# A float32 encoder layer in quads of seven products: subtractions and sums of the up projection, and weight splits, on another engine, and three transfers at other times

## The chip, the cores and the metric

The kernel runs on one core of one Trainium2 chip. A core has a matrix engine (TensorE; PE in the profile, PEld for its weight loads), VectorE (DVE), ScalarE (ACT), GpSimd (POOL), and a sync engine (SP) that here only issues DMAs. Each engine takes its own instructions in the order in which they stand and waits at semaphores. The metric is the device time of one execution in microseconds (us): a median over several runs.

## The reference

One layer of an encoder over 2048 tokens of width 1024, all in float32:

```python
h  = rms_norm(x, norm_mix)
z  = h @ w_in                       # 1024 -> 4352: q_A k_A v_A q_B k_B v_B gate_A gate_B
y_a = windowed_gqa(q_a, k_a, v_a, sink)        # 8 heads on 2 key/value heads, |t-s| <= 128
y_b = neighborhood_attn(q_b, k_b, v_b, rpb)    # 8 heads, 8 x 16 neighbours on a 32 x 64 grid
gates = sigmoid([gate_A, gate_B] + b_gate)
x  = x + (gates_A * (y_a @ w_proj_a) + gates_B * (y_b @ w_proj_b)) @ w_out
x  = x + square(relu(rms_norm(x, norm_mlp) @ w_up)) @ w_down
return rms_norm(x, norm_final)
```

The matrix products of `w_up` (1024 x 4096) and `w_down` (4096 x 1024) take about half of the time.

## The kernel before

**Precision.** A float32 operand goes into TensorE as two numbers of the type float32r: a rounded high part and the rest. `split` makes them: ScalarE casts the high part (L280), and another engine subtracts it from the source (L281). `mm3s` then issues three matmuls (L284 high x high, L285 high x low, L286 low x high). For the slices of weights that the dense tiles use, L176 and L177 do the same.

**Quads.** The input projection, `w_up` and `w_down` are done in quads of two by two blocks with seven products instead of eight, after Strassen and Winograd. The sums of blocks that these need are made by `add` (L277). The `w_up` stage is 16 turns, one quad each (half `m` of the tokens by an eighth `q` of the columns), with its products in the order 1, 5, 6, 2, 7, 4, 3, each for two tiles `a`. Products gather in PSUM banks `b`; VectorE adds them to what is there already (`uc<-b,uc`), ScalarE does relu and square, and after product 3 four more sums (`s1`, `a21`, `s2`, `s4`, L277 too) prepare the left operand of `w_down`, which are stored as `at`.

**The stages by time.** Up to about 365 us the input projection for the first two blocks of tokens' features (`zb`, `zwhl`); from there to 640 the windowed attention A, with dense tiles of the projection (`mm<-hT,whl`) between its units; to 1050 the neighbourhood attention B; to 1440 the gates, the two projections and `w_out`; to 2047 `w_up`; then `w_down`.

**What sets the order.** A planner places the instructions on each engine by a model of their durations, and reads the source's order as a wish only; `tc.issue_after(x)` says that what follows may not be issued before `x`. So an edit at one place can change the order in the whole of its stage.

**Homes.** `pools(stack, side, tags, name)` lays the buffers of a stage out from the left or the right end of SBUF, in the order of the tags. A buffer that comes to lie on one of an earlier stage has to wait for the earlier one's last reader.

**What the change touches.** In `in_left` (L362 ff.) the split of seven left parts of a quad of the input projection; `turned_out` in the loop over the quads, which transposes and stores a quarter of the next block's normalised tokens between products; `qk_tile` and `v_tile`, the dense tiles of attention A's and B's queries, keys and values, with `split_slice` (L176 and L177); `load_kv(g, m)` (L720 ff.), the four DMAs that bring half `m` of the keys and values of group `g` back from DRAM; `began`, a list of the DMAs that bring the queries `qa` of each unit of attention A; the homes of the two attentions; and in `w_up` `up_left` (`uwhla`, `uwhlb`), `up_right` (`ubh`) and `up_quad` (the four sums of `uc`).

## Time and profile before

| | |
|---|---|
| median of 3 runs | 2670.79 us (2670.56 to 2671.09) |
| the profiled execution | 2667.52 us; its span 2665.6 us |
| busy share of the span | PE 97%, PEld 81%, DVE 60%, ACT 46%, POOL 27% |
| mean granted TensorE clock | 0.995 |

The profile is of one execution. A row of a group names the source line, the engine, the operation, the tile that is written and those that are read, how often, busy time and mean duration, and then the idle time of the engine ahead of it with what ended it. A row of the waits names what TensorE stood still for. A row of the timeline gives the start in us from the span's start, the duration, and in brackets the idle time before with its releaser. In a row of the windows stand, for a stretch of time, the busy time of each engine with the number of instructions, the granted clock of TensorE, the busy share of the DMA engines, and what they moved.

### The profile page before, as it was taken

The numbers are of one execution on the slowest core, as the hardware profiler recorded it, in microseconds if no ns is written. First come the engines' busy times: TensorE is split into PE (matmuls) and PEld (weight loads), VectorE is DVE, ScalarE is ACT, GpSimd is POOL, SyncE is SP. The second block draws the span as 40 slices with busy tenths as digits, with TensorE's granted clock in tenths as the row PEclk, the third lists the DMA queues.
The fourth block names the chain that finished last, engine by engine and source line by source line (L and its number), as shares of the span: only waits on it lengthen the run. The fifth ranks groups of instructions, "written<-read, shape, count | busy, mean of one in ns | idle before, by whom it ended". The sixth has DMA issues, their size and how long they took to land. (4 is left out here: it accounts for less than half of the span.)

```text
span 2665.6 us, 34671 instructions
## 1 busy us (share of the span) xinstructions
PE 2596.3 (97%) x12140; PEld 2154.9 (81%) x12140; DVE 1597.4 (60%) x2467; ACT 1238.9 (46%) x2265; POOL 722.5 (27%) x605
## 2 busy tenths in 40 slices
...
GB/s 182 200 156 190 139 248 125 116 117 180 217 218 192 185 181 138 308 160 152 186 182 193 210 202 220 281 188 152 157 115 234 338 113 181 145 146 168 186 190 168
DMA packets 352942, 490.29 MB, mean 184 GB/s; under 512 B 27752, under 2 KB 187624, under 8 KB 350592
## 3 DMA queue, kind: packets, MB, share of 16 engines
...
q14 instruction: 78, 0.64, 0.1%
...
## 5 line engine op out<-in xcount | busy, mean ns | idle before, releaser
L285 PE MATMUL b<-dwh,dah 128*128 128x512 f32 x896 | 348.7, 389 | 0.4 <-DVE dwh L281 0.4
L286 PE MATMUL b<-dwh,dah 128*128 128x512 f32 x896 | 347.7, 389 | 0.0
L284 PE MATMUL b<-dwh,dah 128*128 128x512 f32 x896 | 338.5, 389 | 1.7 <-ACT dwh L280 1.7
L280 ACT CAST dah<-da 128x1024 fp32r<-128x1024 f32 (+1 forms) x128 | 120.8, 945 | 367.6 <-PE b L286 244.6
L277 POOL TENSOR_TENSOR uc<-uc,uc 128x512 f32<-128x512 f32 x120 | 239.7, 2012 | 190.9 <-ACT uc L1204 158.4
L281 DVE TENSOR_TENSOR dah<-da,dah 128x1024 fp32r<-128x1024 f32 (+1 forms) x128 | 139.2, 1089 | 219.5 <-ACT dah L280 216.5
L284 PE MATMUL b<-ubh,uwhlb 128*128 128x512 f32 x592 | 230.6, 390 | 2.7 <-DVE uc L277 1.9
L286 PE MATMUL b<-ubh,uwhlb 128*128 128x512 f32 x592 | 229.7, 390 | 2.3 <-POOL uwhlb L281 1.4
L285 PE MATMUL b<-ubh,uwhlb 128*128 128x512 f32 x592 | 230.4, 389 | 0.0
L200 PE MATMUL mm<-hT,whl 128*128 128x512 f32 x544 | 218.4, 402 | 0.0
L202 PE MATMUL mm<-hT,whl 128*128 128x512 f32 x544 | 214.6, 395 | 0.0
L201 PE MATMUL mm<-hT,whl 128*128 128x512 f32 x544 | 214.2, 394 | 0.0
L284 PEld LDWEIGHTS b<-dwh,dah 128*128 128x128 f32 x896 | 168.1, 188 | 37.0 <-ACT dwh L280 2.1
L284 PE MATMUL zb<-zh,zwhl 128*128 128x512 f32 x476 | 186.9, 394 | 10.4 <-DVE zc L277 7.6
L285 PEld LDWEIGHTS b<-dwh,dah 128*128 128x128 f32 x896 | 168.2, 188 | 35.7 <-DVE dwh L281 0.8
L286 PEld LDWEIGHTS b<-dwh,dah 128*128 128x128 f32 x896 | 168.2, 188 | 34.9
L277 DVE TENSOR_TENSOR uc<-b,uc 128x512 f32<-128x512 f32 x160 | 108.6, 687 | 142.1 <-PE b L286 133.3
L285 PE MATMUL zb<-zh,zwhl 128*128 128x512 f32 x476 | 186.5, 392 | 0.0
L286 PE MATMUL zb<-zh,zwhl 128*128 128x512 f32 x476 | 183.5, 392 | 2.6 <-DVE zwhl L281 2.6
L1452 POOL TENSOR_TENSOR st<-st,power 128x1 f32<-128x1 f32 x16 | 13.6, 857 | 614.5 <-DVE st L1451 614.4
L228 POOL TENSOR_TENSOR st<-st,power 128x1 f32<-128x1 f32 x32 | 23.9, 745 | 470.7 <-DVE st L226 470.6
L284 PEld LDWEIGHTS b<-ubh,uwhlb 128*128 128x128 f32 x592 | 111.1, 188 | 27.2 <-issue 3.1
...
## 6 DMA issues: line engine op xcount, KB each, us to landing
...
```

The costliest lines, as they stand in the source:

```text
L200: PE.matmul(ps, lh, rh, start=first, stop=False)
L201: PE.matmul(ps, lh, rl, start=False, stop=False)
L202: PE.matmul(ps, ll, rh, start=False, stop=last)
L228: G.tensor_tensor(out=r, in0=r, in1=power, op=ALU.pow)
L277: return eng.tensor_tensor(out=out, in0=a, in1=b, op=op).ins
L280: A.copy(hi, src)
L281: return eng.tensor_tensor(out=lo, in0=src, in1=hi.bitcast(F32), op=ALU.subtract).ins
L284: PE.matmul(ps, lh, rh, start=first, stop=False, skip_group_check=True)
L285: PE.matmul(ps, lh, rl, start=False, stop=False, skip_group_check=True)
L286: PE.matmul(ps, ll, rh, start=False, stop=last, skip_group_check=True)
L1452: G.tensor_tensor(out=r, in0=r, in1=power, op=ALU.pow)
```

## The change

Eight edits, in the order of the source.

- `in_left`: the low parts of products 4 and 3 are subtracted on VectorE instead of GpSimd (18 of 128x1024 or smaller).
- The quarters of the next tokens are transposed after the products 2 to 5 of quads 5 and 6 rather than 0 to 3.
- The home of `biasa1` goes from the right side to the left.
- `qk_tile(O_KA)` and `v_tile(O_VA)`: the low part of these two weight slices on VectorE.
- `load_kv` takes an instruction that it is issued after; for the second half it is the load of the queries of unit 8 (for group 0) and 11 (for group 1), counted in the order in which the units run.
- The homes of attention B: `kb0` right behind `masks`, and each of the buffers of `qb` and `biass` a home of its own, in another order.
- `w_up`: products 4 and 3 of the left operand (32 subtractions), the second half of the right operand's pages 4 and 3, and all four sums behind product 3 (120 of 128, eight were there already) on VectorE instead of GpSimd.
- `load_y(b + 1)` stands at another place of the dense stage's source.

```diff
--- before.py
+++ after.py
@@ -387,7 +387,7 @@
                 add(V, s2, a22, a21, ALU.subtract)
             elif n == 3:
                 add(V, a12, a12, s2, ALU.subtract)
-            yield parts({1: a11, 2: a12, 5: s1, 6: s2, 7: a21, 4: a22, 3: a12}[n], G if n in (4, 3) else V)
+            yield parts({1: a11, 2: a12, 5: s1, 6: s2, 7: a21, 4: a22, 3: a12}[n], V)
 
     def v_parts(col, b, vt, p2, v2):
 
@@ -636,8 +636,8 @@
             normalised(xp, xt, Junk(), by_scalar=True)
         ops2.extend(lf if q == 2 else ())
         for n, _ in enumerate(quad2 if q == 2 else in_quad(*QUADS[q], iter(lf), right)):
-            if q in (5, 6) and n < 4:
-                turned_out(h1d[b - 2], in_e().rearrange("p k x -> p (k x)"), xt, n)
+            if q in (5, 6) and 2 <= n < 6:
+                turned_out(h1d[b - 2], in_e().rearrange("p k x -> p (k x)"), xt, n - 2)
     s_z.close()
     s_zp.close()
 
@@ -649,8 +649,8 @@
     s_h = ExitStack()
     hpl = [pool(f"hT{n}", side="left", stack=s_h) for n in range(4)]
     s_a = ExitStack()
-    ap_ = pools(s_a, "left", ("ka1", "va1", "qa", "sta", "sa", "ya", "dist", "ph", "pl"), "a")
-    ap_.update(pools(s_a, "right", ("biasa0", "va0", "ka0", "biasa1"), "a"))
+    ap_ = pools(s_a, "left", ("ka1", "va1", "qa", "sta", "sa", "ya", "dist", "ph", "pl", "biasa1"), "a")
+    ap_.update(pools(s_a, "right", ("biasa0", "va0", "ka0"), "a"))
     hp = {}
 
     def h_pages(b):
@@ -676,7 +676,7 @@
     def qk_tile(col, scale, tiled=False):
         raw = load_slice([(cols(w_in[0], col), KC)])
         yield
-        hl = split_slice(raw)
+        hl = split_slice(raw, V if col == O_KA else G)
         yield
         for b in (2, 3):
             ps = psum("mm", 2)
@@ -689,7 +689,7 @@
     def v_tile(col):
         raw = load_slice([(cols(w_in[0], col), KC)])
         yield
-        hl = split_slice(raw)
+        hl = split_slice(raw, V if col == O_VA else G)
         yield
         for b in (2, 3):
             ps = psum("mm", 2)
@@ -717,12 +717,13 @@
     kas = [T(ap_, [P, 2, S], F32R, f"ka{g}", 1) for g in range(2)]
     vas = [T(ap_, [P, 16, P], F32R, f"va{g}", 1) for g in range(2)]
 
-    def load_kv(g, m):
+    def load_kv(g, m, behind=None):
         k, kd = kas[g][:, :, m * (S // 2) : (m + 1) * (S // 2)], ks_a[m][g]
-        SY.dma_start(k[:, 0].bitcast(F32), kd)
-        SY.dma_start(k[0:64, 1].bitcast(F32), kd[64:128])
-        SY.dma_start(k[64:128, 1].bitcast(F32), kd[0:64])
-        SY.dma_start(vas[g][:, 8 * m : 8 * m + 8].bitcast(F32), vs_a[m][g])
+        with tc.issue_after(behind) if behind else nullcontext():
+            SY.dma_start(k[:, 0].bitcast(F32), kd)
+            SY.dma_start(k[0:64, 1].bitcast(F32), kd[64:128])
+            SY.dma_start(k[64:128, 1].bitcast(F32), kd[0:64])
+            SY.dma_start(vas[g][:, 8 * m : 8 * m + 8].bitcast(F32), vs_a[m][g])
 
     def attn_a(g, i):
         c0, c1 = (1 if i == 0 else 0), (2 if i == 15 else 3)
@@ -834,7 +835,7 @@
     paced(fill, range(12), 24, 3)
     flush(queue=SY)
     for g in range(2):
-        load_kv(g, 1)
+        load_kv(g, 1, began[8 + 3 * g])
     drive((attn_a(g, i) for g in range(2) for i in range(7, 16)), live, True)
     paced(fill, range(12, 24), 24, 3)
     del done[:]
@@ -843,10 +844,10 @@
 
 
     s_b = ExitStack()
-    bp = pools(s_b, "right", ("masks", "qb", "braw0", "biass", "stb", "kb0", "biasl", "braw1", "kb1"), "b")
+    bp = pools(s_b, "right", ("masks", "kb0", "qb0", "braw0", "biass0", "stb", "biass1", "qb1", "qb2", "biasl", "braw1", "kb1"), "b")
     bp.update(pools(s_b, "left", ("sb0", "sb1", "sb2", "vb0", "vb1", "vb2", "phb", "plb", "yb"), "b"))
     boff, bstart, btotal = bias_layout()
-    last_exp, n_raw = [None], [0]
+    last_exp, n_raw, n_short = [None], [0], [0]
     yb = T(bp, [P, BT], F32, "yb", 1)
     masks = T(bp, [P, btotal], F32, "masks", 1)
     with tc.issue_after(began[20]):
@@ -856,7 +857,8 @@
     def make_bias_b(h, jt):
         j = (0, 1, 3)[jt]
         w = B_W[j]
-        t = T(bp, [P, 40 * w], F32, "biasl" if jt == 1 else "biass", 1 if jt == 1 else 2)
+        t = T(bp, [P, 1280 if jt == 1 else 1024], F32, "biasl" if jt == 1 else f"biass{n_short[0] % 2}", 1)[:, : 40 * w]
+        n_short[0] += jt != 1
         raw = T(bp, [P, 512], F32, f"braw{(n_raw[0] + 1) % 2 if n_raw[0] > 1 else 0}", 1)[:, : 16 * w]
         n_raw[0] += 1
         first = h * T_ROWS * w + (T_RO - 11) * w + (B_C0[j] - 16 * j - 15 + T_COFF[j])
@@ -886,7 +888,7 @@
         e, t = h % 2, h // 2
         w, jt = B_W[j], JT[j]
         kp = 4 * w
-        q = T(bp, [P, 4, P], F32R, "qb", 3)
+        q = T(bp, [P, 4, P], F32R, f"qb{n_u % 3}", 1)
         SY.dma_start(q.bitcast(F32), qs_b[t][e][:, :, j])
         yield
         v = T(bp, [P, 8, P], F32R, f"vb{n_u % 3}", 1)
@@ -1099,9 +1101,9 @@
         out[6] = parts(s2, V)
         out[2] = parts(a12, V)
         out[7] = parts(a21, V)
-        out[4] = parts(a22, G)
+        out[4] = parts(a22, V)
         add(V, a12, a12, s2, ALU.subtract)
-        out[3] = parts(a12, G)
+        out[3] = parts(a12, V)
         return out
 
     h2s_d = {n: dp.tile([BT, BT], F32, name=f"h2sum{n}") for n in (5, 6, 7, 4)}
@@ -1146,8 +1148,8 @@
 
         def parts(n, src):
             hi, lo = up_page[n](), up_page[n]()
-            for s, h, l, e in zip(halves(src), halves(hi), halves(lo), (V, G if m and n in (4, 3) else V)):
-                last = split(s, h, l, e)
+            for s, h, l in zip(halves(src), halves(hi), halves(lo)):
+                last = split(s, h, l, V)
             right[n] = (hi, lo)
             page_done[0] = last
 
@@ -1253,14 +1255,13 @@
                     last = plus(a21, ps, a21)
                     squared(a21)
                     s1, s2, s4 = up_rings["c"](), up_rings["c"](), up_rings["c"]()
-                    e = V if m == 1 and q == 7 else G
-                    add(e, s1, a21, a22)
+                    add(V, s1, a21, a22)
                     keep(5, a, s1)
-                    add(e, a21, a11, a21, ALU.subtract)
+                    add(V, a21, a11, a21, ALU.subtract)
                     keep(7, a, a21)
-                    add(e, s2, s1, a11, ALU.subtract)
+                    add(V, s2, s1, a11, ALU.subtract)
                     keep(6, a, s2)
-                    add(e, s4, a12, s2, ALU.subtract)
+                    add(V, s4, a12, s2, ALU.subtract)
                     keep(3, a, s4)
             if last:
                 with tc.issue_after(last):
@@ -1330,6 +1331,8 @@
         for t in range(4):
             row0 = b * BT + t * P
             xt = load_tile(p4x, "xr", 5, xf[row0 : row0 + P])
+            if t == 1 and b < NB - 1:
+                next_y = load_y(b + 1)
             for c in range(2):
                 xc = xt[:, c * BT : (c + 1) * BT]
                 ps = psum("pt", 2)
@@ -1341,8 +1344,6 @@
             put(x2d[b][t * P : (t + 1) * P], xt)
             tiles.append(xt)
         flush()
-        if b < NB - 1:
-            next_y = load_y(b + 1)
         normalised(p4x, tiles, Unused())
     h2 = T(p4x, [P, KC, BT], F32R, "mh", 1).bitcast(F32)
     for g in range(4):
```

In instruction rows VectorE goes from 2442 to 2613 and GpSimd from 508 to 334. TensorE's order is the same from the middle of the first turn of `w_up` on to the end, and in the whole dense stage from about 1050 to 1440 us, where the orders of the other engines are the same too; the last edit moves nothing there. The places where it changes are around 74 to 130, 215 to 295, 353 to 433 and 640 to 880 us and at the start of `w_up`. Three of them are shown.

SP's queue, around 385 to 400 us, where attention A's units begin. `ka0` and `ka1` are the keys of the two groups, `ks_a0` and `ks_a1` the first and second half of them in DRAM, `qa_...` a unit's queries. Before:

```order
L735 DMA qa_322_3116<-qs_a10_78 128x4x128
L686 DMA ks_a1_81<-z_432_3918 64x2x512 x2
L735 DMA qa_332_3187<-qs_a10_78 128x4x128
L686 DMA ks_a1_81<-z_433_3948 64x2x512 x2
L722 DMA ka0_291_2936<-ks_a1_81 128x1024
L723 DMA ka0_291_2936<-ks_a1_81 64x1024
L187 DMA raw_444_4095<-in_w_in_dram 128x8x128
L724 DMA ka0_291_2936<-ks_a1_81 64x1024
L722 DMA ka1_292_2937<-ks_a1_81 128x1024
L723 DMA ka1_292_2937<-ks_a1_81 64x1024
L735 DMA qa_342_3258<-qs_a10_78 128x4x128
```

Now:

```order
L736 DMA qa_332_3187<-qs_a10_78 128x4x128
L736 DMA qa_342_3258<-qs_a10_78 128x4x128
L686 DMA ks_a1_81<-z_433_3948 64x2x512 x2
L187 DMA raw_444_4095<-in_w_in_dram 128x8x128
L736 DMA qa_352_3329<-qs_a10_78 128x4x128
L173 DMA y_a1_103<-ya_321_3113 64x4x128
L736 DMA qa_363_3405<-qs_a00_76 128x4x128
L701 DMA vs_a1_83<-z_437_3986 128x2x512
L736 DMA qa_373_3476<-qs_a00_76 128x4x128
L723 DMA ka0_291_2936<-ks_a1_81 128x1024
L724 DMA ka0_291_2936<-ks_a1_81 64x1024
L725 DMA ka0_291_2936<-ks_a1_81 64x1024
```

The loads of the second half's keys stood ahead of `qa_342` and `qa_352`; now four more loads of queries stand ahead of the first of them, and those of `ka1` come some dozen rows later still.

VectorE's queue around 346 to 360 us, the end of the input projection: `hT` are the pages of normalised tokens for the dense tiles, `zc` the sums that empty the PSUM banks `zb`, `zwhl` and `whl` weights. Before:

```order
L667 SCALAR_TENSOR_TENSOR hT_287_2921<-raw_288_2922,g_mix_68,hT_286_2920 128x512 x2
L667 SCALAR_TENSOR_TENSOR hT_287_2921<-raw_289_2928,g_mix_68,hT_286_2920 128x512 x2
L277 TENSOR_TENSOR zc_278_2707<-zb_76_2694,zc_274_2621 128x512
L277 TENSOR_TENSOR zc_279_2722<-zb_77_2709,zc_275_2636 128x512
L667 SCALAR_TENSOR_TENSOR hT_299_2948<-raw_300_2949,g_mix_68,hT_298_2947 128x512 x2
L277 TENSOR_TENSOR zc_280_2736<-zb_76_2694,zc_274_2621 128x512
L277 TENSOR_TENSOR zc_280_2736<-zb_74_2668,zc_280_2736 128x512
L277 TENSOR_TENSOR zc_281_2752<-zb_77_2709,zc_275_2636 128x512
```

Now:

```order
L667 SCALAR_TENSOR_TENSOR hT_287_2921<-raw_288_2922,g_mix_68,hT_286_2920 128x512 x2
L667 SCALAR_TENSOR_TENSOR hT_287_2921<-raw_289_2928,g_mix_68,hT_286_2920 128x512 x2
L277 TENSOR_TENSOR zc_278_2707<-zb_76_2694,zc_274_2621 128x512
L281 TENSOR_TENSOR zwhl_272_2601<-zraw_256_2375,zwhl_272_2601 128x1024
L177 TENSOR_TENSOR whl_296_2942<-raw_295_2940,whl_296_2942 128x1024
L277 TENSOR_TENSOR zc_279_2722<-zb_77_2709,zc_275_2636 128x512
L177 TENSOR_TENSOR whl_306_2975<-raw_297_2945,whl_306_2975 128x1024
L281 TENSOR_TENSOR zwhl_273_2605<-zraw_256_2375,zwhl_273_2605 128x1024
L667 SCALAR_TENSOR_TENSOR hT_299_2948<-raw_300_2949,g_mix_68,hT_298_2947 128x512 x2
L277 TENSOR_TENSOR zc_280_2736<-zb_76_2694,zc_274_2621 128x512
```

Four subtractions of weights (L281 and L177), which were GpSimd's, stand between the first `zc` and the `hT` that follow.

VectorE's queue at the start of `w_up`, around 1445 to 1460 us: `ubh2`, `ubh4`, `ubh3` are pages of the right operand, `uwhl...` the left one's parts, `uc_1585<-b_5` and `uc_1586<-b_6` the sums that empty two PSUM banks. Before:

```order
L281 TENSOR_TENSOR ubh2_1570_13557<-urb_1568_13554,ubh2_1569_13556 128x1024 x2
L277 TENSOR_TENSOR urb_1568_13554<-urb_1568_13554,uraw_1538_13158 128x1024 x2
L281 TENSOR_TENSOR ubh4_1574_13571<-urb_1568_13554,ubh4_1573_13570 128x1024 x2
L277 TENSOR_TENSOR uc_1585_13716<-b_5_13642,uc_1579_13599 128x512
L277 TENSOR_TENSOR uc_1586_13734<-b_6_13657,uc_1580_13614 128x512
L281 TENSOR_TENSOR ubh3_1576_13577<-uraw_1565_13542,ubh3_1575_13576 128x1024
L277 TENSOR_TENSOR uc_1585_13716<-b_3_13616,uc_1585_13716 128x512
L281 TENSOR_TENSOR ubh3_1576_13577<-uraw_1565_13542,ubh3_1575_13576 128x1024
L281 TENSOR_TENSOR uwhlb_1593_13824<-uraw_1577_13582,uwhlb_1593_13824 128x1024
L277 TENSOR_TENSOR uc_1586_13734<-b_4_13629,uc_1586_13734 128x512
```

Now:

```order
L281 TENSOR_TENSOR ubh2_1570_13569<-urb_1568_13566,ubh2_1569_13568 128x1024 x2
L277 TENSOR_TENSOR urb_1568_13566<-urb_1568_13566,uraw_1538_13170 128x1024 x2
L281 TENSOR_TENSOR ubh4_1574_13583<-urb_1568_13566,ubh4_1573_13582 128x1024 x2
L281 TENSOR_TENSOR ubh3_1576_13589<-uraw_1565_13554,ubh3_1575_13588 128x1024 x2
L281 TENSOR_TENSOR uwhlb_1593_13836<-uraw_1577_13594,uwhlb_1593_13836 128x1024
L277 TENSOR_TENSOR uS_1594_13839<-uraw_1577_13594,uraw_1578_13596 128x1024
L277 TENSOR_TENSOR uc_1585_13728<-b_5_13654,uc_1579_13611 128x512
L277 TENSOR_TENSOR uc_1586_13746<-b_6_13669,uc_1580_13626 128x512
L281 TENSOR_TENSOR uwhla_1551_13209<-uraw_1536_13166,uwhla_1551_13209 128x1024
```

TensorE's queue at the same place, before:

```order
L285 MATMUL b_2_13601<-ubh2_1570_13557,uwhla_1548_13187 128x512
L286 MATMUL b_2_13601<-ubh2_1569_13556,uwhla_1548_13187 128x512
L284 MATMUL b_5_13642<-ubh4_1573_13570,uwhlb_1550_13193 128x512
L285 MATMUL b_5_13642<-ubh4_1574_13571,uwhlb_1550_13193 128x512
L286 MATMUL b_5_13642<-ubh4_1573_13570,uwhlb_1550_13193 128x512
```

Now:

```order
L285 MATMUL b_2_13613<-ubh2_1570_13569,uwhla_1548_13199 128x512
L286 MATMUL b_2_13613<-ubh2_1569_13568,uwhla_1548_13199 128x512
L286 MATMUL b_7_13870<-ubh1_1539_13173,uwhlb_1593_13836 128x512
L284 MATMUL b_7_13870<-ubh1_1539_13173,uwhlb_1593_13836 128x512
L285 MATMUL b_7_13870<-ubh1_1540_13174,uwhlb_1593_13836 128x512
```

On VectorE both halves of `ubh3`, the low part of `uwhlb_1593` and a sum now stand ahead of the two that empty `b_5` and `b_6`. On TensorE the products with `uwhlb_1593` (`b_7`, and `b_8` behind it) now come directly behind `b_2`; before, product 4 (`ubh4`, `b_5`) did.

## The prediction

> **What bounds the kernel now.** I read the page's first part, then the waits of TensorE, then windows of the stretches in which it waits, then the timeline there.
>
> ```profile
> PE 2596.3 (97%) x12140; PEld 2154.9 (81%) x12140; DVE 1597.4 (60%) x2467; ACT 1238.9 (46%) x2265; POOL 722.5 (27%) x605
> ...
> PE s L742 <- DMA qa<-qs_a: 9.3, 1, 9.3
> PE zb L284 <- DVE zc L277: 7.6, 3, 3.4
> ...
> PE b L284 <- DVE uc L277: 5.1, 4, 2.0
> ...
> PE zb L286 <- DVE zwhl L281: 2.6, 3, 1.4
> PE s L903 <- DMA kb<-ks_b: 2.5, 2, 1.6
> ...
> PE b L286 <- POOL uwhlb L281: 1.4, 1, 1.4
> ```
>
> TensorE bounds it: 2596.3 of 2665.6 us, and no matmul is added or taken away. What can be won is some of the other 69 us, and time at a lower clock. The rows of the waits (total, times, longest) say that there is one long wait for queries, and many of 1 to 3 us for VectorE. The windows say where:
>
> ```profile
> core 0: us, PE busy (x) PEld busy (x) DVE busy (x) ACT busy (x) POOL busy (x), PEclk, DMA share, GB/s
> 66.00:110.00 44.00, 42.58 (x190) 34.90 (x191) 34.59 (x41) 14.63 (x19) 10.52 (x5) 1.00 0.65 201
> 264.00:280.00 16.00, 11.80 (x52) 9.16 (x51) 9.22 (x21) 6.69 (x10) 5.35 (x3) 1.00 0.70 195
> 340.00:365.00 25.00, 21.62 (x89) 17.49 (x89) 16.59 (x21) 11.92 (x17) 9.92 (x4) 0.93 0.69 223
> 392.00:412.00 20.00, 9.90 (x45) 7.74 (x44) 9.07 (x31) 10.16 (x34) 5.18 (x10) 0.74 0.81 174
> 606.00:702.00 96.00, 90.75 (x472) 75.10 (x473) 53.32 (x142) 55.18 (x138) 43.94 (x52) 1.00 0.64 178
> 1130.00:1140.00 10.00, 7.99 (x29) 6.39 (x29) 5.49 (x9) 3.94 (x7) 0.56 (x1) 0.83 0.62 203
> 1440.00:1456.00 16.00, 12.97 (x55) 9.77 (x54) 15.64 (x15) 8.76 (x12) 0.60 (x2) 1.00 0.96 253
> 1490.00:1533.00 43.00, 40.61 (x177) 32.68 (x176) 27.89 (x26) 22.93 (x35) 23.62 (x12) 1.00 0.64 220
> 1533.00:1720.00 187.00, 186.95 (x825) 154.42 (x824) 129.66 (x112) 89.29 (x128) 103.31 (x50) 1.00 0.64 223
> 1720.00:1768.00 48.00, 43.06 (x179) 33.96 (x178) 38.49 (x28) 27.12 (x38) 32.67 (x14) 0.96 0.74 263
> ```
>
> In the steady part of w_up (1533 to 1720) TensorE loses 0.05 of 187 us. It loses 4.9 in 1720 to 1768, 2.4 in 1490 to 1533, 3.0 in 1440 to 1456, 10.1 in 392 to 412. The column PEclk shows a second loss: 0.93 of 25 us, 0.96 of 48 and 0.83 of 10 are about 3.4 us at half speed each, so 1.7 us of work, each behind a wait.
>
> **The prices.** What VectorE pays for the moved work, and what GpSimd's work costs VectorE:
>
> ```profile
> L277 DVE TENSOR_TENSOR uc<-uc,uc 128x512 f32<-128x512 f32 x8 | 5.3, 690 | 0.1
> L277 POOL TENSOR_TENSOR uc<-uc,uc 128x512 f32<-128x512 f32 x120 | 239.7, 2012 | 190.9 <-ACT uc L1204 158.4 <-DMA at<-uc 27.9
> L277 DVE TENSOR_TENSOR uc<-b,uc 128x512 f32<-128x512 f32 x158 | 107.2, 687 | 142.1 <-PE b L286 133.3 <-issue 5.7 <-POOL uc L277 1.8
> L281 DVE TENSOR_TENSOR uwhlb<-uraw,uwhlb 128x1024 fp32r<-128x1024 f32 x30 | 59.3, 1975 | 13.5 <-ACT uwhlb L280 13.5
> ...
> 1736.58 1.22 DVE L281 TENSOR_TENSOR ubh<-uraw,ubh 128x1024 fp32r<-128x1024 f32 x1
> ...
> 1741.08 0.68 DVE L277 TENSOR_TENSOR uc<-b,uc 128x512 f32<-128x512 f32 x1
> ...
> 1746.67 2.31 DVE L277 TENSOR_TENSOR uS<-uraw,uraw 128x1024 f32<-128x1024 f32 x1
> ...
> 1760.05 1.27 DVE L277 TENSOR_TENSOR uc<-b,uc 128x512 f32<-128x512 f32 x2
> ...
> 1455.00:2046.00 591.00, 583.20 (x2554) 479.34 (x2552) 384.51 (x324) 286.05 (x406) 323.80 (x154) 1.00 0.55 193
> ```
>
> A sum of 128x512 takes 0.69 us on VectorE (the eight already there) and 2.01 on GpSimd. A 128x1024 operation takes VectorE 1.22 us when GpSimd stands idle (1736.58) and 2.31 beside its sums (1746.67); the mean of 30 splits in w_up is 1.98. So VectorE takes on 120 x 0.69 + 32 x 1.22 = 122 us there, and gets back at most 1.0 us on each of some 150 such operations, by the mean above nearer 0.65, so about 100 us. Its 384.5 of 591 us become some 410, 69%, and it has 133 us of waiting for TensorE ahead of the sums that empty the banks (`uc<-b,uc`, whose 0.69 us GpSimd does not stretch).
>
> **Part 1, to 300 us.** The 18 splits on VectorE and the later quarters. At 98 us a wait of 1.4 for a low part of `zwhl` may go (VectorE is busy 34.6 of 44 us). The 4.2 us lost in 264 to 280 hang on the chain from the next tokens' loads through ScalarE to the transposes, which only stands elsewhere. I take 0.5 us of gain, from -1.5 to +4.
>
> **Part 2, 340 to 365.**
>
> ```profile
> 346.07 4.80 POOL L177 TENSOR_TENSOR whl<-raw,whl 128x1024 fp32r<-128x1024 f32 x2
> 350.83 2.79 POOL L281 TENSOR_TENSOR zwhl<-zraw,zwhl 128x1024 fp32r<-128x1024 f32 x1
> ...
> 349.99 4.18 DVE L667 SCALAR_TENSOR_TENSOR hT<-raw,g_mix,hT 128x512 fp32r<-128x512 f32 x2 [3.15 <-ACT hT L666]
> 354.10 2.00 DVE L277 TENSOR_TENSOR zc<-zb,zc 128x512 f32<-128x512 f32 x3
> ...
> 354.92 0.75 PE L284 MATMUL zb<-zh,zwhl 128*128 128x512 f32 x1 [3.38 <-DVE zc L277]
> ```
>
> TensorE waits for `zc`, which waits behind two `hT` that took 4.18 us beside GpSimd's splits. Those splits now stand behind the first `zc` on VectorE. A 128x512 operation that is not stretched takes about 0.7 us, so the two `hT` end at 351.5 to 351.8 and `zc` at about 352.5 instead of 354.8. Two splits, 2.4 us, come ahead of the second `zc`, and TensorE has 12 matmuls, 2.7 us, for the first bank meanwhile. The wait of 3.38 falls to about 1.3, and I take it as too short for the half-speed stretch: 2.1 + 1.7 = 3.8 us of gain (from 0 to 5).
>
> **Part 3, the keys.**
>
> ```profile
> 391.35 0.64 SPq L735 DMA_DIRECT2D qa<-qs_a  x1
> ...
> 402.52 0.66 PE L742 MATMUL s<-ka,qa 128*128 128x384 f32 x1 [9.27 <-DMA qa<-qs_a]
> ```
>
> `qa_342` is issued at 391.35 behind loads of the second half's keys and lands 11 us later. Now it is issued right behind `qa_332`, and the queries of four units stand ahead of the first such load. The 9.3 us go, and with them 3.6 us of work at half speed behind 402.5 (PEclk 0.74 over 20 us), 1.8 us. Late next is `ka0`'s second half itself: its load is now held back, and whoever needs it stands behind the units whose queries go ahead of it. For that and for short waits within those units, which now stand closer together, I leave 1 us: gain 10, from 4 to 11.
>
> **Part 4, the change of attentions.** 606 to 702 loses 5.2 us, 2.5 of it for `kb`, whose home now comes free earlier. The order of 640 to 880 is new throughout, with short waits for `phb` or `plb` that can appear anew. I take 0, from -3 to +3.
>
> **Part 5, the start of w_up, which loses.**
>
> ```profile
> 1449.26 2.36 DVE L281 TENSOR_TENSOR ubh<-urb,ubh 128x1024 fp32r<-128x1024 f32 x2
> 1451.54 1.28 DVE L277 TENSOR_TENSOR uc<-b,uc 128x512 f32<-128x512 f32 x2
> ...
> 1452.09 2.00 ACT L280 CAST ubh<-uraw 128x1024 fp32r<-128x1024 f32 x2 [1.24 <-DMA h2d<-mh]
> ...
> 1450.61 0.39 PE L285 MATMUL b<-ubh,uwhla 128*128 128x512 f32 x1
> 1450.84 0.39 PE L286 MATMUL b<-ubh,uwhla 128*128 128x512 f32 x1
> 1452.37 0.47 PE L284 MATMUL b<-ubh,uwhlb 128*128 128x512 f32 x1 [1.14 <-DVE uc L277]
> ```
>
> The cast of `ubh3` waits until 1452.09 for the stores of `mh`, whose home it has, while the DMA engines are 96% busy. Before, VectorE emptied `b_5` and `b_6` in the meantime, and TensorE went on at 1452.37. In the new order both halves of `ubh3` stand ahead of `uwhlb_1593`, and TensorE's next products need that one's low part. The casts end at 1453.1 and 1454.1, the low parts of `ubh3` at 1454.3 and 1455.4, that of `uwhlb_1593` at 1456.6. TensorE stands from 1451.2 to 1456.7: 5.5 us instead of 1.1. The 68 matmuls up to the first row that both orders share are the same, and take 15.4 us at 0.227 each (0.23 between the two rows from 1450.61) in either order: so 4.4 lost, and 1.7 if half speed follows, as behind the 3.38 above. I take -6, from -2 (the stores land early) to -8.
>
> VectorE is busy 15.64 of 16 us here. The Trainium skill ("Perfetto Trace Analysis", Optimizing Scalar/DVE Operations) says that with VectorE saturated, handing work to GpSimd may make sense, which speaks against taking it back here; but it adds that the two share a read port, so that it might not help. By the first half two more splits would cost at least 2.4 us here; the 2.31 against 1.22 us bear the second out, and the sum above goes by the order.
>
> **Part 6, the rest of w_up.** 2.4 us at 1490 to 1533 and 4.9 at 1720 to 1768, with 1.7 for the clock, are 9.0. The first is a wait for GpSimd's `uwhlb` itself, which goes. In the second VectorE worked from 1741.08 to 1760.05 between two emptyings. The new order has 11 operations of 128x1024 and 8 sums there. Back to back they stand 1.14 and 0.60 apart (two `ubh` of 1.22 in 2.36 us at 1449.26, two sums of 0.68 in 1.28 at 1451.54): 12.5 + 4.8 = 17.3 us against 19.0. Since TensorE will also come there earlier, one wait of about 2 us and perhaps 1 elsewhere stays. Gain 6, from 2 to 9.
>
> The skill ("TensorE: Matmul & The Clock Gate", Part 1) puts half speed behind at least about 3.4 us without work. By that a wait of 2.0 us would cost no clock, and part 6 would win 1.7 less; the window 1130 to 1140, PEclk 0.83 behind a loss of 2.0 us, says that it does cost it.
>
> **The sum.** The dense stage and w_down keep their orders: 0. 0.5 + 3.8 + 10 + 0 - 6 + 6 = 14.3 us off 2667.5, the profiled execution: 2653.2. The median of the runs shown is 3.3 above that one: 2656.5, said as 2656.
>
> **The rivals.**
> The start of w_up is free: the stores of `mh` land in time, or the casts find other room. Then part 5 is near 0, and with the better ends of parts 1 and 4 the time is about 2647. For it: 1.14 us is all that TensorE lost there. Against it: DMA share 0.96. Chance 0.15.
> The queries' wait moves: the first half's or second half's keys, now later, are what a unit waits for, with the same 11 us from issue to landing. Part 3 falls to 0 and the time is 2666. For it: a busy queue, 0.81 in 392 to 412. Against it: four units' queries stand between. Chance 0.13.
> The change doesn't do what it says: GpSimd isn't what stretches VectorE. Then VectorE has 384.5 + 122 us in w_up's 591, parts 2 and 6 win nothing, and it is about 2666. The 1.22 and 2.31 us ten microseconds apart speak against it. Chance 0.04.
> Slower: VectorE's queue. In each turn eight sums, 4.8 us, now stand in order with those that empty banks. If in each of the 15 turns behind the first one the emptying of a bank comes 2.4 us (four sums) late for TensorE, 36 us are lost and the time is 2692; it decides from 1.0 us in a turn on (15 us, all the gain), and from 1.3 the kernel is slower by over 0.2%. For it: VectorE near 70%. Against it: 133 us of waiting ahead of 158 emptyings, 0.84 each, and the stretch goes. Chance 0.08.
>
> **How the numbers follow.** The forecast has 0.60, its own range 2649 to 2662. With the rivals on both sides 8 in 10 lie within 2646 to 2667. About 0.2% (5.3 us) is what a measurement of this kernel can tell from no change. Faster: 0.57 of the forecast, 0.15, and 0.07 of the two at 2666: 0.79. Within 0.2%: 0.12. Slower: the last rival and a little of parts 4 and 5 worse than their bounds: 0.09.
>
> **What would show it.** Right: no wait for `qa` near 400 us; the wait near 355 at 1 to 1.5 us with PEclk 1.00; VectorE's 128x1024 operations in w_up at 1.22 us; a wait of 4 to 6 us of TensorE for VectorE's `uwhlb` 10 to 15 us into w_up, the longest of that stage. Wrong: waits of TensorE for `uc` in every turn, a wait for `ka`, or a new one of over 3 us between 640 and 880.

## The result, and the profile after

The changed kernel takes 2644.62 us (median of 5 runs, 2644.13 to 2649.04) against 2670.56 of the kernel before in the same comparison (5 runs, 2670.3 to 2671.09): a ratio of 0.9906 with a 95% interval of 0.9892 to 0.9921. That is 25.9 us less; the prediction said 2656, with a range of its own from 2649 to 2662, and from 2646 to 2667 with the rivals. The profiled execution lies on the median, 2644.62 us with a span of 2642.5.

The first row of the page of the kernel after, and four rows of TensorE's waits (total, times, longest):

```profile
PE 2590.5 (98%) x12140; PEld 2150.9 (81%) x12140; DVE 1627.2 (62%) x2641; ACT 1240.4 (47%) x2265; POOL 350.5 (13%) x431
...
PE b L286 <- DVE uwhlb L281: 6.2, 1, 6.2
PE zb L284 <- DVE zc L277: 3.4, 2, 3.0
...
PE s L743 <- DVE sta L745: 1.9, 3, 1.1
...
PE b L284 <- ACT uc L1235: 1.6, 1, 1.6
```

The 9.3 us for `qa` and the wait for GpSimd's `uwhlb` are gone, and of the 2.5 us for `kb` 0.5 are left; the 6.2 us for VectorE's `uwhlb` are new. The 3.0 us for `zc` are those near 267 us, which part 1 of the prediction took as staying. GpSimd's busy time halved, 722.5 to 350.5 us, while VectorE's rose by only 29.8. Its splits in `w_up`, 1.98 us in the mean before, now take 1.22:

```profile
L281 DVE TENSOR_TENSOR uwhlb<-uraw,uwhlb 128x1024 fp32r<-128x1024 f32 x48 | 58.7, 1222 | 39.1 <-ACT uwhlb L280 39.0
```

The windows of the kernel after, laid where the same work now stands:

```profile
core 0: us, PE busy (x) PEld busy (x) DVE busy (x) ACT busy (x) POOL busy (x), PEclk, DMA share, GB/s
...
338.00:363.00 25.00, 24.55 (x111) 19.85 (x110) 19.74 (x27) 12.93 (x18) 1.02 (x2) 1.00 0.90 273
385.00:405.00 20.00, 19.53 (x114) 16.63 (x113) 15.73 (x52) 15.96 (x45) 9.85 (x17) 1.00 0.56 160
...
1011.00:1021.00 10.00, 8.35 (x40) 6.69 (x39) 6.20 (x10) 6.98 (x12) 2.39 (x1) 0.83 0.50 171
...
1424.00:1446.00 22.00, 14.52 (x55) 11.30 (x56) 18.69 (x20) 9.92 (x14) 0.00 (x0) 0.84 0.96 285
1473.00:1516.00 43.00, 43.00 (x191) 35.64 (x190) 30.21 (x38) 22.59 (x34) 0.00 (x0) 1.00 0.73 249
1516.00:1703.00 187.00, 187.00 (x826) 154.90 (x826) 133.10 (x164) 91.11 (x128) 1.19 (x1) 1.00 0.64 225
1703.00:1751.00 48.00, 46.38 (x205) 38.07 (x205) 37.18 (x43) 29.79 (x40) 0.00 (x0) 1.00 0.76 268
1440.00:2026.00 586.00, 583.08 (x2569) 481.94 (x2567) 398.61 (x479) 290.06 (x410) 1.19 (x1) 1.00 0.55 193
```

TensorE stands 0.5 of 25 us at the end of the input projection, 0.5 of 20 where the queries were waited for, nothing at 1473 to 1516, and 1.6 of 48 at the change of `w_up`'s halves. It stands 7.5 of 22 us at the start of `w_up`. The PEclk of 0.84 there is 6.8 us at half speed; 3.9 of them fall into the wait itself, and the 2.9 behind it cost about 1.5 us of work. It stands 1.65 us at 1011 to 1021, with half speed behind it (0.83 of 10 us).

All kernels issue 12140 matmuls, so the start of the n-th one in a profile, less that of the n-th one before, says how much has been won or lost up to there. This table is worked out from the profiles of all runs but the first additions, which fell into the dense stage (us; what a kernel is, stands below):

```
n-th matmul           1200   1500   1700   2000   3200   5000   5200   5600   6800   6900   7500   8000   8500  12139
at, in before        287.0  360.2  411.7  473.3  712.1 1021.2 1057.8 1152.8 1428.3 1455.2 1594.7 1708.4 1829.6 2657.1
after                 -1.0   -5.6  -16.4  -19.3  -21.5  -20.0  -15.8  -18.7  -19.5  -13.1  -16.5  -16.9  -22.9  -22.9
keys alone             1.0    2.1   -7.6   -7.5   -7.0   -7.1   -7.1   -9.1   -4.7   -4.8   -4.6   -4.9   -3.5   -3.5
after, keys undone    -1.9   -5.7  -17.2  -20.2  -22.3  -20.8  -16.5  -19.6  -17.2  -10.3  -13.8  -14.2  -20.2  -20.2
w_up's edits alone     4.8    3.2    5.8    6.1    5.9    5.9    5.9    3.3    3.3    3.3    1.8    1.4   -4.6   -4.6
after, w_up undone    -0.9   -4.8  -16.4  -19.3  -21.4  -19.0  -14.8  -17.4  -17.4  -17.4  -15.9  -16.1  -17.2  -16.0
early splits alone     3.6   -0.2  -11.3  -14.2  -13.8  -14.2  -14.2  -17.5  -17.7  -17.7  -16.9  -16.9  -17.5  -17.5
homes alone            2.9    4.0    4.4    4.7    3.1    4.5    8.8    6.0    5.3    5.2    6.3    6.1    4.2    4.2
sums alone             3.1    1.5    4.2    4.4    6.6    6.5    6.5    4.0    4.4    4.4    1.2    0.8   -7.1   -7.1
w_up's splits alone    5.6    5.5    8.3    8.4    7.9    7.9    7.8    5.3    7.8    7.8   10.2   12.7   10.8   10.8
first turn back       -0.7   -4.5  -16.1  -19.0  -21.2  -19.6  -15.5  -19.1  -19.7  -19.7  -22.5  -22.9  -28.8  -28.8
additions, half two    0.4   -3.5  -15.0  -17.9  -20.0  -18.0  -13.4  -15.8  -13.5   -6.9  -10.4  -10.8  -16.7  -16.7
additions, change     -0.9   -5.6  -16.4  -19.4  -20.5  -19.0  -16.5  -18.7  -19.7  -13.0  -16.5  -16.9  -12.2  -12.2
less                   1.8   -1.9  -13.5  -16.4  -17.5  -17.9  -17.9  -20.8  -18.4  -18.5  -21.7  -22.1  -28.0  -28.0
two pieces             0.8   -3.8  -14.3  -17.2  -18.1  -18.5  -18.5  -20.9  -21.0  -21.0  -24.2  -24.6  -32.5  -32.5
```

The row of the kernel after by stretches: 1.0 us up to the 1200th matmul, 4.6 to the 1500th, 10.8 to the 1700th and 2.9 more to the 2000th, 0.7 between the 2000th and the 5000th in sum, 4.2 lost to the 5200th, 3.7 won to the 6800th, 6.4 lost to the 6900th, 9.8 won to the 8500th. Behind it, nothing. One warning stands in the same table: from the 5200th to the 5600th all fourteen kernels shown here won 2.0 to 3.6 us against the profiled execution of before, whatever was changed in them. There it was that one execution which waited longer (the PEclk of 0.83 at 1130), so these 3 us are no part of the change. The other way round, the five kernels with before's order up to the 1200th matmul stood 1.0 to 5.6 us behind that execution there.

### The profile page after: what moved, and what is told of

The parts are those of the page before. It is cut to its first block, busy times and chain, and to the rows that moved or that the text cites. A ratio compares the mean times of both kernels' runs of the same rounds, so it can differ in the third digit from the quotient of the medians.

```text
span 2642.5 us, 34515 instructions
## 1 busy us (share of the span) xinstructions
PE 2590.5 (98%) x12140; PEld 2150.9 (81%) x12140; DVE 1627.2 (62%) x2641; ACT 1240.4 (47%) x2265; POOL 350.5 (13%) x431
## 4 chain that ended last, share of the span: by engine, by line
PE 86%; DVE 5%; DMA 4%; ACT 3%; issue 1%; SPq 1%; POOL 0%; ACTq 0%; DVEq 0%; POOLq 0%
PE b L286 15%; PE b L285 15%; PE b L284 15%; PE mm L200 5%; PE mm L202 5%; PE mm L201 5%; PE zb L286 3%; PE zb L284 3%; PE zb L285 3%; PE av L944 2%; PE pt L200 2%; PE pt L201 2%; PE pt L202 2%; PE pt L933 2%; PE s L905 2%
## 5 line engine op out<-in xcount | busy, mean ns | idle before, releaser
L281 DVE TENSOR_TENSOR dah<-da,dah 128x1024 fp32r<-128x1024 f32 (+1 forms) x128 | 139.3, 1090 | 215.9 <-ACT dah L280 212.7
L1453 POOL TENSOR_TENSOR st<-st,power 128x1 f32<-128x1 f32 x16 | 13.5, 857 | 937.1 <-DVE st L1452 937.0
L286 PEld LDWEIGHTS b<-ubh,uwhlb 128*128 128x128 f32 x592 | 111.5, 188 | 29.6 <-DVE uwhlb L281 6.7
L284 PEld LDWEIGHTS b<-ubh,uwhlb 128*128 128x128 f32 x592 | 111.5, 188 | 26.6 <-ACT uc L1235 2.0
L285 PEld LDWEIGHTS b<-ubh,uwhlb 128*128 128x128 f32 x592 | 111.4, 188 | 23.4
```

What stands on the lines that cost most here:

```text
L281: return eng.tensor_tensor(out=lo, in0=src, in1=hi.bitcast(F32), op=ALU.subtract).ins
L284: PE.matmul(ps, lh, rh, start=first, stop=False, skip_group_check=True)
L285: PE.matmul(ps, lh, rl, start=False, stop=False, skip_group_check=True)
L286: PE.matmul(ps, ll, rh, start=False, stop=last, skip_group_check=True)
```

## Experiments: the keys' loads

**Keys alone**: before, with one edit.

```diff
...
-        load_kv(g, 1)
+        load_kv(g, 1, began[8 + 3 * g])
```

> The kernel before with one edit: the second half's keys are issued behind the queries of units 8 and 11. If the place of these loads in SP's queue makes the wait for queries, as part 3 of the prediction has it, the wait of 9.27 us near 402 goes with its half-speed stretch, and with luck the one near 443 as well: 10 to 14 us, 2657 to 2661. If it goes only because VectorE and GpSimd share their work in another way, under 3 us: 2668 or more.

Measured: 2659.95 us against 2670.85, ratio 0.9951 (0.9934 to 0.9968). The wait for `qa` is gone, 9.7 us between the 1500th and the 1700th matmul. A wait of 1.81 us for `pl`, at 434.8 here and at 442.66 in before, stays with its half speed.

**After, keys undone**: the same two lines the other way round, all else as changed.

> The changed kernel with that one edit undone. TensorE, VectorE, ScalarE and GpSimd keep the changed kernel's order; SP's queue alone differs, around 385 to 450 us. By part 3 of the prediction a wait for queries of about 9 us comes back: 2654 to 2657. By the rival, that the other edits alone take the wait away (queries stand ahead of keys by the new order anyway), it stays at 2644 to 2647.

Measured: 2647.45 us, ratio 0.991 (0.9895 to 0.9925). The wait does not come back: the row of the table falls to -17.2 at the 1700th matmul like that of after. So the loads' place is enough to take the wait away, but in the changed kernel something else takes it away as well.

**Early splits alone**: before, with the splits of the input projection and of the key and value columns on VectorE.

```diff
-            yield parts({...}[n], G if n in (4, 3) else V)
+            yield parts({...}[n], V)
...
-        hl = split_slice(raw)
+        hl = split_slice(raw, V if col == O_KA else G)
...
-        hl = split_slice(raw)
+        hl = split_slice(raw, V if col == O_VA else G)
```

> The kernel before with the weight splits of the in-projection (parts 4 and 3 of each quad, and the key and value columns) on VectorE; the loads of the second half's keys stay where they were. Theory: the wait of 3.38 us near 355 falls to at most 1.5 us and its half speed goes, 3 to 4 us. For the wait for the queries near 402 the two theories differ. If only the place of the key loads in the queue matters (what I predicted), the 9.3 us stay, and the time is about 2666. If a split on VectorE moves the queries ahead of the keys as well, as the run of the changed kernel without that edit suggests, the wait is gone, and the time is about 2654 to 2657.

Measured: 2648.5 us against 2673.23, ratio 0.991 (0.9898 to 0.9923). This one piece wins 24.7 us in the medians, nearly what the whole change does. SP's queue in before (first two rows) and then here (last two):

```profile
381.56 0.68 SPq L735 DMA_DIRECT2D qa<-qs_a  x1
...
387.70 0.32 SPq L722 DMA_DIRECT2D ka<-ks_a  x1
```

```profile
379.17 6.29 SPq L735 DMA_DIRECT2D qa<-qs_a  x2
...
388.86 0.32 SPq L722 DMA_DIRECT2D ka<-ks_a  x1
```

With the splits moved, the planner puts two loads of queries, not one, ahead of the second half's keys, and nobody waits. By these rows the wait is a matter of one row's place in a queue, and two edits of this change each move that row. The gain at 340 to 365 comes with this edit alone too (3.6 to -0.2 at the 1500th matmul, 3.8), and 2.9 us go from the 1700th to the 2000th matmul: the wait of 1.81 us, which the prediction left out, with the half speed behind it. The timeline of before there:

```profile
439.53 2.36 POOL L177 TENSOR_TENSOR whl<-raw,whl 128x1024 fp32r<-128x1024 f32 x1 [4.18 <-ACT whl L176]
...
439.82 2.10 DVE L748 TENSOR_TENSOR sta<-sink_t,sta 128x4 f32<-128x4 f32 x1
...
441.83 0.68 DVE L765 TENSOR_TENSOR pl<-pt,ph 128x512 fp32r<-128x512 f32 x1
...
442.66 0.63 PE L761 MATMUL pt<-ident,sa 128*128 128x128 f32 x4 [1.81 <-DVE pl L765]
```

An operation on 128x4 numbers takes 2.10 us beside GpSimd's split, and `pl`, for which TensorE waits, stands behind it.

## Experiments: the start and the rest of w_up

**w_up's edits alone** and **after, w_up undone**: before with the hunks of `up_left`, `up_right` and `up_quad`, and after without them.

> The kernel before with the edits in w_up alone. By the two traces, matched at common rows, w_up's start loses 6.3 us and its rest wins 9.6: net 3.3, so 2667, with the same wait of about 6 us for uwhlb near the start. If the loss at the start hangs on what came before it in time, the wait is not there and the kernel is at about 2661.

> The changed kernel with the edits in w_up undone. If the parts add up: 2644.6 + 3.3, about 2648, no wait at w_up's start, and waits of 7 to 9 us for GpSimd and VectorE in the rest of w_up. If the edits in w_up are what the gain comes from: 2660 or more.

Measured: 2662.54 us, ratio 0.9963 (0.995 to 0.9976), and 2651.11 us, ratio 0.9924 (0.9909 to 0.9939). The edits win 7.9 us of their own between the 6800th and the 8500th matmul, and undoing them gives back the rest of `w_up`'s gain. But neither kernel loses anything at the start of `w_up` (0.0 from the 6800th to the 6900th matmul in both); with the edits of `w_up` alone, VectorE still has the two sums ahead of `ubh3`. The loss of 6.4 us there needs the edits of `w_up` together with those of the stages ahead.

In the kernel after it looks as the prediction drew it:

```profile
1437.96 0.79 PE L286 MATMUL b<-ubh,uwhlb 128*128 128x512 f32 x1 [6.25 <-DVE uwhlb L281]
...
1434.41 2.36 DVE L281 TENSOR_TENSOR ubh<-uraw,ubh 128x1024 fp32r<-128x1024 f32 x2 [2.27 <-ACT ubh L280]
1436.68 1.22 DVE L281 TENSOR_TENSOR uwhlb<-uraw,uwhlb 128x1024 fp32r<-128x1024 f32 x1
1437.82 1.22 DVE L277 TENSOR_TENSOR uS<-uraw,uraw 128x1024 f32<-128x1024 f32 x1
1438.95 1.28 DVE L277 TENSOR_TENSOR uc<-b,uc 128x512 f32<-128x512 f32 x2
```

VectorE waits for ScalarE's casts of `ubh3`, does both halves, then `uwhlb` and a sum, and the two sums that empty the banks start at 1438.95, 4.5 us after the first of these.

**First turn back**: after, with the splits of parts 4 and 3 on GpSimd in the first turn alone. VectorE then has the two sums ahead of `ubh3` again, and TensorE product 4 directly behind `b_2`.

```diff
-    def up_left(ws, behind=None):
+    def up_left(ws, behind=None, late=V):
...
-        out[4] = parts(a22, V)
+        out[4] = parts(a22, late)
...
-        out[3] = parts(a12, V)
+        out[3] = parts(a12, late)
...
-        started.extend((rights, up_left(ws)))
+        started.extend((rights, up_left(ws, late=G)))
```

> The changed kernel with two splits of the first turn of w_up, parts 4 and 3 of its weights, back on GpSimd; everything else stays. The order of VectorE at the start of w_up then has the two sums that empty b_5 and b_6 ahead of the halves of ubh3 again. Theory (the order of VectorE's queue makes the start of w_up stand): TensorE's wait of 6.25 us near 1438 falls to two waits of about 1.2 us, no half-speed stretch follows it, and the time falls by 4 to 6 us, to about 2640. Rival (the late stores of mh make it stand, in whatever order): a wait of 4 us or more stays there, and the time stays within 2 us of 2644.6.

Measured: 2641.78 us against 2673.23, ratio 0.9887 (0.9872 to 0.9901). From the 6800th to the 6900th matmul nothing is lost, and at the end the profile is 5.9 us ahead of after's. The casts of `ubh3` wait for the stores of `mh` as in after, where they start at 1433.33. ScalarE, VectorE and TensorE here:

```profile
1432.89 2.00 ACT L280 CAST ubh<-uraw 128x1024 fp32r<-128x1024 f32 x2 [1.72 <-DMA h2d<-mh]
...
1431.86 1.28 DVE L277 TENSOR_TENSOR uc<-b,uc 128x512 f32<-128x512 f32 x2
...
1432.69 0.47 PE L284 MATMUL b<-ubh,uwhlb 128*128 128x512 f32 x1 [1.15 <-DVE uc L277]
```

So the stores are as late, and it was the new order that made TensorE stand, not the stores. The run brings back the order on VectorE and that on TensorE together, so it doesn't show which of the two would have been enough. By the rows of after VectorE's would: the sums that empty the banks start 7 us later there, and product 4 needs them too.

**Sums alone** and **w_up's splits alone**: before with one of the two pieces each.

```diff
-                    e = V if m == 1 and q == 7 else G
-                    add(e, s1, a21, a22)
+                    add(V, s1, a21, a22)
...
```

```diff
-        out[4] = parts(a22, G)
+        out[4] = parts(a22, V)
...
-            for s, h, l, e in zip(halves(src), halves(hi), halves(lo), (V, G if m and n in (4, 3) else V)):
-                last = split(s, h, l, e)
+            for s, h, l in zip(halves(src), halves(hi), halves(lo)):
+                last = split(s, h, l, V)
```

> The kernel before with the 120 sums of w_up on VectorE alone; the weight splits of w_up stay on GpSimd, and all outside w_up stays. Theory (the sums, GpSimd's longest work there, are what costs): from the 6900th to the 8500th matmul it wins 7 us or more of the 7.8 that the kernel with all edits of w_up won there. Rival (the splits that TensorE waits for are what costs, as the wait of 1.4 us for GpSimd's uwhlb suggests): it wins at most 3 us there.

> The kernel before with the 32 weight splits of w_up on VectorE alone; the sums stay on GpSimd. Theory (the sums are what costs): VectorE gets 32 more operations of 128x1024 that GpSimd's sums stretch to about 2 us, 64 us more in w_up, and nothing is won: from the 6900th to the 8500th matmul 0 to 8 us slower than before. Rival (the splits are what costs): 3 us or more faster there.

Measured: 2658.77 us, ratio 0.9954 (0.994 to 0.9968), and 2672.58 us, ratio 1.0008 (0.9998 to 1.0018). From the 6900th to the 8500th matmul the sums alone win 11.5 us, more than all three edits together (7.9), and the splits alone lose 3.0, in the slowest of that kernel's ten executions. So the sums on GpSimd were the whole cost there, and the 32 splits of `w_up` belong to no gain at all. With the sums on VectorE they even cost: the five kernels with sums and splits there (after, keys undone, w_up's edits alone, first turn back, less) win 7.9 to 9.9 us in this stretch, and all five wait 1.62 us for `uc` at the change of halves; the two with the sums but without the splits (sums alone, two pieces) win 11.5 and don't wait.

## Experiments: does GpSimd's work stretch VectorE's, and does it cost?

**Additions, first try**: after, with work for GpSimd that nobody uses.

```diff
                     add(V, s4, a12, s2, ALU.subtract)
                     keep(3, a, s4)
+                    with tc.issue_after(last):
+                        for _ in range(16):
+                            add(G, ident, ident, ident, ALU.mult)
```

> The changed kernel, in which GpSimd multiplies a 128x128 tile of zeros and ones with itself 16 times behind each pair of squared halves in w_up, 512 times in all; nobody uses the result, and VectorE, ScalarE and TensorE keep the order of the changed kernel there. Theory (GpSimd's work beside it is what stretches VectorE's 128x1024 operations): their mean in w_up rises from 1.22 us to 1.5 or more, and TensorE gets short waits for sums and splits back, of 2 to 8 us in all. Rival (before was slow for its longer chain of waits between the engines, not for the stretch): they stay at 1.22 us, and the time stays within 2 us of the changed kernel's.

Measured: 2673.61 us, ratio 1.001 (1.0001 to 1.0019), 29.0 above after. But not where it was meant to: the planner moved the multiplications ahead of `w_up`, to 1037 to 1354 us, most of them into the dense stage. For the question it is a miss. What it measured instead: GpSimd's busy queue delays what it does for others. Three rows of it, a wait of TensorE and two groups in the dense stage:

```profile
PE pt L200 <- DVE xr L1345: 13.0, 6, 8.2
```

```profile
1124.54 10.46 POOL L277 TENSOR_TENSOR ident<-ident 128x128 f32<-128x128 f32 x22
1134.96 0.56 POOL L228 TENSOR_TENSOR st<-st,power 128x1 f32<-128x1 f32 x1
```

```profile
L177 DVE TENSOR_TENSOR whl<-raw,whl 128x1024 fp32r<-128x1024 f32 x25 | 33.9, 1358 | 19.1 <-ACT whl L176 16.9 <-DMA raw<-in_w_proj_b_dram 2.1
```

A 128x1 operation stood behind 22 multiplications, 10.5 us, and TensorE waited 8.2 us at the end of that chain. VectorE's splits there took 1.36 us, against 1.22 in after.

**Additions, half two**: additions tied to the data, in the second half of `w_up` alone.

```diff
                     add(V, s4, a12, s2, ALU.subtract)
                     keep(3, a, s4)
+                    if m == 1:
+                        G.tensor_scalar(out=warm, in0=s4[:, 0:1], scalar1=0.0, scalar2=1.0, op0=ALU.mult, op1=ALU.add)
+                        spare = up_rings["chunk"]()
+                        G.memset(spare, 0.0)
+                        G.tensor_scalar(out=spare[:, 0:1], in0=spare[:, 0:1], scalar1=warm, scalar2=None, op0=ALU.mult)
+                        for _ in range(4):
+                            add(G, spare, spare, spare)
```

> The changed kernel, in which GpSimd, in the second half of w_up alone, sets an idle 128x512 tile to zero behind each pair of sums and adds it to itself four times (64 additions of 128x512, the size that was taken from it); nobody uses the result. TensorE's order stays, VectorE's but for 23 rows; the first half of w_up is the control. Theory (GpSimd's additions beside it stretch VectorE's 128x1024 operations): VectorE's 128x1024 operations rise from 1.22 us to a mean of 1.6 or more in the second half and stay at 1.22 in the first, and TensorE waits longer there, by 1 to 6 us. Rival (nothing is stretched by another engine; before was slow for its chains of waits): 1.22 us in both halves, and the time stays within 1.5 us of the changed kernel's 2644.6.

Measured: 2646.1 us, ratio 0.9913 (0.9898 to 0.9927), 1.5 above after. Groups of VectorE, of the first half of `w_up` (one row), and of the second (three rows):

```profile
L281 DVE TENSOR_TENSOR uwhlb<-uraw,uwhlb 128x1024 fp32r<-128x1024 f32 x25 | 30.5, 1222 | 13.8 <-ACT uwhlb L280 13.6
```

```profile
L277 DVE TENSOR_TENSOR uc<-b,uc 128x512 f32<-128x512 f32 x77 | 51.8, 687 | 51.3 <-PE b L286 50.8
...
L281 DVE TENSOR_TENSOR uwhlb<-uraw,uwhlb 128x1024 fp32r<-128x1024 f32 x24 | 35.4, 1474 | 18.1 <-ACT uwhlb L280 18.1
...
L277 DVE TENSOR_TENSOR uraw<-uraw,uS 128x1024 f32<-128x1024 f32 x8 | 15.6, 1955 | 0.0
```

The stretch is real: 1.22 us in the control half, 1.47 and 1.96 beside the additions. The mean over all 79 operations of 128x1024 there, 1.48 (117.2 us in seven groups), is below the 1.6 that the theory said. And TensorE did not pay for it: from the 8000th to the 8500th matmul this kernel wins 5.9 us where after wins 6.0, and from there on its row of the table doesn't move. The 6.2 us by which its profile lies behind after's come ahead of `w_up` (6.0 at the 6800th). VectorE had time to spare in that half, and an operation that takes longer there costs nothing that shows.

**Additions, change**: the same kind of additions, sixteen, only in the last turn of the first half, so that they fall on VectorE's fullest 25 us.

```diff
                     squared(c1[a])
                     keep(2, a, c1[a])
+                    if (m, q) == (0, 7):
+                        G.tensor_scalar(out=warm, in0=c1[a][:, 0:1], scalar1=0.0, scalar2=1.0, op0=ALU.mult, op1=ALU.add)
...
+                        for _ in range(8):
+                            add(G, spare, spare, spare)
```

> The changed kernel, in which GpSimd makes 16 additions of 128x512 that nobody uses in the last turn of w_up's first half alone, behind the squares of its part 4, so that they fall beside VectorE's fullest stretch, some 20 us before the second half. TensorE's order stays; nine rows of VectorE differ, as in the kernel with the additions in the whole second half, which is the control. Theory (where VectorE has no idle time, the stretch itself is what TensorE waits for): VectorE's 128x1024 operations rise there from 1.22 us to about 2, and of the 6 us that the changed kernel won from the 8000th to the 8500th matmul at least 3 go. Rival (the sums cost before since they were late on GpSimd, with those that wait for them behind): the operations are stretched, but those 6 us stay within 1.5.

Measured: 2659.42 us against 2671.47, ratio 0.9953 (0.9938 to 0.9968): 14.8 above after, from 16 additions; in the profiles it is 10.7, all of it at this place. The timeline there, VectorE, TensorE and then ScalarE:

```profile
1726.85 1.21 DVE L277 TENSOR_TENSOR uS<-uraw,uraw 128x1024 f32<-128x1024 f32 x1
...
1734.60 2.05 DVE L277 TENSOR_TENSOR uraw<-uraw,uS 128x1024 f32<-128x1024 f32 x1
1736.58 2.97 DVE L277 TENSOR_TENSOR uc<-uc,uc 128x512 f32<-128x512 f32 x2
1739.47 2.06 DVE L281 TENSOR_TENSOR uwhla<-uraw,uwhla 128x1024 fp32r<-128x1024 f32 x1
```

```profile
1736.26 0.80 PE L284 MATMUL b<-ubh,uwhlb 128*128 128x512 f32 x1 [3.75 <-ACT uc L1235]
1748.79 0.79 PE L284 MATMUL b<-ubh,uwhla 128*128 128x512 f32 x1 [4.30 <-DVE uc L277]
```

```profile
1735.62 0.59 ACT L1235 COPY uc<-b 128x512 f32<-128x512 f32 x1 [2.03 <-DMA at<-uc]
...
1738.18 0.58 ACT L1235 COPY uc<-b 128x512 f32<-128x512 f32 x1 [1.97 <-DVE uc L277]
```

Operations of 1.21 us take 2.05, two sums of 1.28 take 2.97, and TensorE waits 3.75 and 4.30 us. Where after won 6.0 us from the 8000th to the 8500th matmul, this kernel loses 4.7, with the same order on TensorE, and on VectorE the order of the control. So the stretch itself is enough to make TensorE wait at this place. In before too, TensorE's four waits there are for VectorE, none for GpSimd's sums: 1.18 us near 1723, 0.81 near 1741, and these two:

```profile
1753.49 0.50 PE L286 MATMUL b<-ubh,uwhlb 128*128 128x512 f32 x1 [0.94 <-DVE uwhlb L281]
...
1760.78 0.50 PE L284 MATMUL b<-ubh,uwhla 128*128 128x512 f32 x1 [2.01 <-DVE uc L277]
```

What before paid for the stretch is not the 10.7 us, though. In this run the sums of `uc` are VectorE's and are stretched as well, and the first wait runs through one of them: a copy of ScalarE's waits for the store of a sum.

The Trainium skill ("SBUF — State Buffer", Who interferes with whom) says that a VectorE operation with both inputs in SBUF shares a port with GpSimd's reads, and that one with at most one input in SBUF, outside the two-port modes, does not. The rows agree: `uc<-uc,uc` and the splits are stretched, `uc<-b,uc`, which reads a PSUM bank, stays at 0.69.

## Experiments: the homes, and less of the change

**Homes alone**: before, with the new homes at the change of attentions.

```diff
...
-    bp = pools(s_b, "right", ("masks", "qb", "braw0", "biass", "stb", "kb0", "biasl", "braw1", "kb1"), "b")
+    bp = pools(s_b, "right", ("masks", "kb0", "qb0", "braw0", "biass0", "stb", "biass1", "qb1", "qb2", "biasl", "braw1", "kb1"), "b")
...
```

> The kernel before with the new homes at the change of attentions alone (biasa, masks, kb, qb, biass). Theory (they are what cost the changed kernel 4.2 us near the 5100th matmul, at 1016 us, and won 1 to 2 us between 640 and 700): both show here as well, 1 to 2 us won up to the 3200th matmul and 3 to 5 lost from the 5000th to the 5200th; the time is 1 to 4 us above before's, within what before itself varies. Rival (the loss at 1016 came from the other edits, which bring the second attention's end against other loads): nothing is lost there, and the time is at or 1 to 3 us below before's.

Measured: 2672.03 us, ratio 1.0008 (0.9997 to 1.0019). By the table 1.6 us are won from the 2000th to the 3200th matmul, and 4.3 lost from the 5000th to the 5200th. The row of TensorE in this kernel, and the one in after:

```profile
1040.73 0.39 PE L943 MATMUL av<-phb,vb 128*128 128x256 f32 x1 [1.28 <-ACT phb L937]
```

```profile
1016.14 0.39 PE L944 MATMUL av<-phb,vb 128*128 128x256 f32 x1 [1.22 <-ACT phb L938]
```

It is the same wait at the end of attention B, and the homes make it. They are attention B's: in less, below, where `biasa1` alone has its new home, nothing is lost there. Why `phb` comes later with them was not looked at. Of the 4.2 us, 1.9 are waits (2.1 in sum, 0.2 in before) and 1.7 half speed (PEclk 0.83 over 10 us); the remaining 0.6 isn't accounted for.

**Less**: after with the first turn's two splits on GpSimd, and without the later quarters and attention B's new homes (`biasa1`'s stays new). **Two pieces**: before with the early splits and the sums, so the hunks of those two experiments and nothing else.

> The changed kernel with the first turn's two splits back on GpSimd, and without the later quarters and the new homes of the second attention (masks, kb, qb, biass as before). Theory (those two edits win nothing: part 4 of the prediction at 0): at least as fast as the kernel with the two splits back alone, up to 4 us faster, about 2636 to 2640, since the wait of 3.0 us near 267 and short waits between 640 and 1020 shrink. Rival (the homes win the 2.5 us of waits for kb): 2 to 4 us slower than that one, with waits for kb back near 690.

> The kernel before with two pieces of the change alone: the weight splits of the in-projection and of the key and value columns on VectorE, and the 120 sums of w_up on VectorE. Left as before: the splits of w_up, the loads of the second half's keys, the quarters, the homes and y's pages. Theory (these two pieces win all there is, some 22 to 25 and 8 to 12 us of their own, at different places; the rest costs about 10 us at the start of w_up and at 1016 us): 2634 to 2640 us, below the changed kernel and at or below the 2638.7 of the kernel with the two splits of the first turn back and without the homes. Rival (the pieces win the same time twice, or the splits of w_up on GpSimd cost beside VectorE's sums): 2643 or more.

Measured: 2638.73 us against 2673.23, ratio 0.9874 (0.9859 to 0.9888), and 2638.86 us against 2671.47, ratio 0.9883 (0.9867 to 0.99). The first interval lies below that of after (0.9892 to 0.9921), the second reaches 0.0008 into it. The waits of the second:

```profile
PE zb L274 <- DVE xin L237: 8.0, 2, 7.4
PE zb L284 <- ACT zwhl L280: 4.4, 1, 4.4
PE mm L200 <- ACT whl L176: 3.5, 2, 2.3
PE s L742 <- DVE sta L744: 1.9, 3, 1.1
```

There is no wait for `qa`, none for the low part of `uwhlb`, and from 280 us to the last ten no stretch at half speed. Two pieces of the change win as much as the whole, or a little more. Both take work from GpSimd where VectorE has no time to spare, and the first also moves a load in SP's queue. The rest wins nothing in the total, and costs 6.4 us at the start of `w_up` and 4 at the end of attention B. Two small gains of it show in the profiles: the homes alone win 1.6 us from the 2000th to the 3200th matmul, and the quarters seem to win some 2 near 268 us. That the kernel without the homes and quarters is faster than the one with them (2638.7 to 2641.8) lies within the intervals. On the quarters alone there was no run. But TensorE's wait near 268 us is 2.9 to 3.4 us in the seven profiles with the early splits and the later quarters, and 3.9 to 4.7, for a cast of `zwhl`, in the three with the early splits and the old quarters (early splits alone, less, two pieces). For the move of `load_y` and of `biasa1` alone there was no run either.

## Why the prediction was right or wrong

The direction was right and the gain too small: 14.3 us off the profiled execution were said, 23.1 came (span 2665.6 to 2642.5). What failed is the size of two terms, part 3 and part 6, each short by 3.7 to 3.8 us, and part 4, which had 0 where 3.5 were lost. By its own steps:

- **Part 1**, 0.5: 1.0 by the table, which is less than what executions differ by there. The wait at 98 us that it named is what the early splits win: 1.2 to 1.7 us in all six profiles without them, none in the ten with them. The waits at 264 to 280 stay, as said.
- **Part 2**, 3.8: 4.6 up to the 1500th matmul, and 3.8 with the splits alone. The wait left is 0.36 us (1.15 with the splits alone), not 1.3: a pair of unstretched `hT` takes 1.41 us, and the next `zc` stands only one pair behind.
- **Part 3**, the keys, 10: 13.7 between the 1500th and the 2000th. The 9.3 and the half speed went as said (10.8); the failed step is what stood behind. The prediction has no term for the 1.81 us at 442.66 and the half speed behind them, and they went too (2.9); "For that and for short waits within those units, which now stand closer together, I leave 1 us" took time off instead. It also gave the whole to the loads' place. The early splits take both waits away, the loads' place only that for `qa`; and up to the 5000th matmul the changed kernel without the edit of the loads is 0.8 us ahead of the one with it, so that edit wins nothing there on top.
- **Part 4**, 0, from -3 to +3: 2.2 won up to the 3200th matmul, then 1.5 and 4.2 lost. The last is where the failed step lies: the prediction looked at "2.5 of it for `kb`" and named new waits for `phb` or `plb` within 640 to 880 us as possible. They came at the end of attention B, at 1016, with the moved homes, and with half speed behind them.
- **Part 5**, the start of `w_up`, -6: -6.4, with a wait of 6.25 us where 5.5 was said. The mechanism is shown by the run with the first turn back.
- **Part 6**, 6, from 2 to 9: 9.8. Mis-sized on both sides. The prediction counted 9.0 us lost in before, 7.3 of idle time and 1.7 for the clock. By the starts of TensorE's matmuls, 0.227 us apart when nothing holds them up, before lost 11.5 us from the 6900th to the 8500th. The matmuls overlap (0.39 us each), so the idle time in a profile shows each wait some 0.3 us short, 2.4 us in all. And of "one wait of about 2 us and perhaps 1 elsewhere stays", 1.7 stayed. Two pieces, without the splits, lost nothing there. The count of VectorE's work was right: 398.6 of 586 us, 68%, where 69% was said.
- **The sum**: 0 for the dense stage. 3 of its 3.7 us were the bad luck of before's profiled execution there, and no effect of the change. The other 0.8 isn't accounted for. The forecast also added 3.3 us, since before's profiled execution lay that much below the median; after's lies on its median. So of the 11.9 us by which the forecast missed, 4.9 are in the six parts, 3.7 in the dense stage and 3.3 in this. Where those 3.3 us lie no run shows.

Of the rivals none came. The queue of VectorE did not become the bound; the run with `w_up`'s splits alone, which lost 3.0 us with GpSimd's sums still beside it, is the nearest to it. On half speed the rows went against the rule of the Trainium skill again ("TensorE: Matmul & The Clock Gate", Part 1, at least about 3.4 us without work): at 1016 us two waits of 1.22 and 0.43 were followed by a PEclk of 0.83.
